# Scores of two attention mixers as stacked one-pass products, and rotations with one shuffle

## The chip, the cores and the metric

The kernel runs on one core of a Trainium2 chip. The metric is the device time of one execution in microseconds (us). Names of engines in the profile: PE is TensorE's matrix unit, PEld its weight loads, DVE VectorE, ACT ScalarE, POOL GpSimd, SP the engine that issues most transfers.

## The reference

A bidirectional encoder trunk with two layers, width 1024, on 256 grid tokens (4 rows by 64 columns) and 16 meta tokens, 272 in all. A layer is half a SwiGLU block, a mixer, and half a SwiGLU block again, each ahead of it an RMS norm. The mixer runs three attentions on one combined projection:

```python
def hybrid_mixer(n, w_in, sink, rpb, qn, kn, w_branch, w_out, pos, row, col):
    ...
    ang = rope_angles(pos, HEAD_DIM)
    oa = window_sink_attention(apply_rope(heads(qa, A_Q_HEADS), ang), apply_rope(heads(ka, A_KV_HEADS), ang),
                               heads(va, A_KV_HEADS), sink)
    ob = neighbourhood_attention(heads(qb, B_HEADS), heads(kb, B_HEADS), heads(vb, B_HEADS), rpb)
    qc = apply_axial_rope(rms_norm(heads(qc, C_Q_HEADS), qn), row, col)
    kc = apply_axial_rope(rms_norm(heads(kc, C_KV_HEADS), kn), row, col)
    oc = dense_block_attention(qc, kc, heads(vc, C_KV_HEADS))
    branches = jnp.stack([oa, ob, oc], axis=2)
    up = jnp.einsum('blnc,ncd->blnd', branches, w_branch)
    g = jax.nn.sigmoid(gates.reshape(B, L, N_BRANCH, D_MODEL))
    return jnp.sum(g * up, axis=2) @ w_out
```

A and C have 8 query heads and 2 key heads of 64 dimensions, B has 8 of each. A is a window of 128 positions with a sink logit per head, C is dense. apply_rope turns dimension d of the first half of a head with dimension d of its second half:

```python
    return jnp.concatenate([x1 * cos - x2 * sin, x2 * cos + x1 * sin], axis=-1).astype(x.dtype)
```

apply_axial_rope does the same in each half of a head (32 dimensions), by row and by column.

## The kernel before, in words

Tokens run along the free dimension (T = 272 columns; 256 in what follows the last layer's mixer inputs), features along the 128 partitions. Projections are made in three one-pass products (fp32r): weights and activations are each split into a rounded part (hi, xh) and the rest (lo, xl), and mm (L267 to L280) sums hi·xh, hi·xl and lo·xh into a tile acc. unit (L217) loads a block of weights of 4 x 128 rows by 256 columns (raw), ScalarE makes hi by a copy that rounds, and VectorE, in the mixer for every third block POOL, makes lo by a subtraction. With pairs=True it also reorders the columns so that one head of each key group lie next to each other: group g = 0 in partitions 0 to 63 of a projection's output, g = 1 in 64 to 127; then ScalarE works in two halves, and the rest is made half by POOL and half by VectorE (L232).

The mixer (L681) projects B's values, keys and queries first. Then weave (L861) runs an attention and, at each of its yields, one piece of other work: beside neighbourhood (B) the pieces a_keys, a_queries(0), a_queries(1) and c_keys, beside mix_a c_queries(0), c_queries(1) and three or four gated(1, mp), beside mix_c the gated(0, mp), and then gated(2, mp) and the output projection. A scheduler puts each engine's instructions in an order of its own, with the program's order as its guide; each engine then runs its queue in that order.

The queries of A and C are in one tile of 128 partitions x 4 heads x 272 (qa, qc), the keys in one of 128 x 272 (ka, kc), both in full fp32. grouped (L466) computes the scores: products (L474) makes four heads at a time, each by one fp32 product with 64 rows, which leaves two records on TensorE:

```python
                PE.matmul(s, q[g * HD:(g + 1) * HD, t, qi * 128:(qi + 1) * 128], kk[g * HD:(g + 1) * HD, :],
                          start=True, stop=True)
```

Each product writes one of three PSUM banks (bank("s", 3)), which transposes use too; a bank is free again when the softmax pass on VectorE (L402 in A and B, L407 in C) or, in C, ScalarE's exponential (L409) has read it. turned (L496) transposes the probabilities, values (L509) makes the weighted sums. There are 2 query blocks x 2 halves x 4 heads = 16 such products per mixer and layer. meta_products (L520) does the same for the 16 meta queries of all heads at once, in layer 0 only.

rope_a (L737) makes A's rotation: four products of 32 partitions each read one quarter of the projection and write it, times the sine, to the quarter that it is turned with (L742), one product with the cosine (L743), and POOL adds (L744). rope_c (L779) makes the tables from cosine, sine and gain on VectorE at each of its three calls (L783, L784), shuffles by 16 partitions within 32 (L785), and multiplies and adds on POOL and VectorE.

qk (L156) gives buffers of a pool with six of 128 x 1408, which biases, vb, kb, qb, qa, qc, the running sums of the gated branches (tot) and the split inputs of the output projection (halves) take in turn; scr (L113) gives one of five of 128 x 544.

## Time and profile before

| | us |
|---|---|
| median of 3 runs | 1351.46 (1351.28 to 1352.11) |
| profiled execution | 1346.27 |
| its span | 1344.5 |
| VectorE busy | 890.4 |
| ScalarE busy | 649.5 |
| POOL busy | 159.5 |
| attention of layer 0, from the transposes of B's values to the last weighted sum | about 248 to 430 |
| attention of layer 1, the same | about 926 to 1075 |

Busy times are of one profiled execution. A record on PE lasts about 0.29 us for a projection product, but these are pipelined: the next starts after about 0.125 us. What a product costs is therefore read from start to start, not from its duration. The timeline gives the start of each record from the start of the span; records of one line in a row are merged with their count.

### The profile page before, as it was taken

The page shows a single profiled execution, that of the slowest core. Times are in us where ns is not written, and L with a number is a line of the kernel's source. Part 1 is how long each engine was busy: PE and PEld are TensorE (multiplying, and loading weights), DVE is VectorE, ACT ScalarE, POOL GpSimd, SP SyncE. Part 2 cuts the span into 40 slices and gives each one's busy share as a digit, 9 for nine tenths or more (in the row PEclk, how much of TensorE's full clock was granted, in tenths as well). Part 3 has the DMA queues.
Part 4 walks back from the last instruction along what each step waited for, and adds up shares of the span by engine and source line. Part 5 has one row for each costly group of instructions (what it writes and reads, how often), then busy time and mean ns, then how long its engine had stood idle before and what let it go on. Part 6 is the DMA issues. An engine that isn't in the chain of part 4 may idle for free.

```text
span 1344.5 us, 25887 instructions
## 1 busy us (share of the span) xinstructions
PE 1326.9 (99%) x10683; PEld 1286.6 (96%) x10683; DVE 890.4 (66%) x1316; ACT 649.5 (48%) x937; POOL 159.5 (12%) x97
## 2 busy tenths in 40 slices
PE   9999999999999999999999999999999999999997
PEld 8999999988988999999999999999889999999997
DVE  6655669688564687646676646676886557765663
ACT  6443444455454455434455434454565545544444
POOL 1000001232122220000000000023321233000000
PEclk9999999998999999999999999999999999999998
DMA  7765556433334576555465555455334465566652
GB/s 231 209 185 174 181 169 191 141 107 95 110 112 125 171 201 185 175 178 179 156 192 173 173 176 179 157 180 157 110 95 122 122 180 184 182 189 188 188 173 78
DMA packets 239010, 217.52 MB, mean 162 GB/s; under 512 B 24804, under 2 KB 237980, under 8 KB 238764
## 3 DMA queue, kind: packets, MB, share of 16 engines
q1 hardware_dynamic: 238540, 215.20, 52.4%
q8 instruction: 84, 1.38, 0.4%
q10 hardware_dynamic: 352, 0.66, 0.1%
q14 instruction: 34, 0.28, 0.1%
HBM read 214.78 MB, written 1.05 MB: 161 GB/s over the span
## 4 chain that ended last, share of the span: by engine, by line
PE 93%; DVE 5%; ACT 1%; issue 1%; DMA 0%; ACTq 0%; DVEq 0%
PE acc L279 29%; PE acc L280 28%; PE acc L278 28%; PE s L479 2%; PE pv L437 2%; PE s L502 1%; DVE lo L235 1%; PE s L641 1%; PE pv L432 1%; DVE p L422 1%; PE s L653 1%; PE s L337 0%; DMA qk<-in_meta_tokens_dram 0%; DVE p L402 0%; ACT hi L234 0%
## 5 line engine op out<-in xcount | busy, mean ns | idle before, releaser
L234 ACT CAST hi<-raw 128x1024 fp32r<-128x1024 f32 (+1 forms) x390 | 402.6, 1033 | 564.6 <-PE acc L279 384.9
L279 PE MATMUL acc<-xl,hi 128*128 128x272 f32 (+1 forms) x2160 | 622.5, 288 | 0.0
L280 PE MATMUL acc<-xh,lo 128*128 128x272 f32 (+1 forms) x2160 | 620.2, 287 | 0.7 <-DVE lo L235 0.7
L278 PE MATMUL acc<-xh,hi 128*128 128x272 f32 (+1 forms) x2160 | 619.9, 287 | 0.6 <-DVE qk L722 0.6
L235 DVE TENSOR_TENSOR lo<-raw,hi 128x1024 fp32r<-128x1024 f32 (+1 forms) x352 | 428.2, 1217 | 216.3 <-ACT hi L234 215.9
L278 PEld LDWEIGHTS acc<-xh,hi 128*128 128x128 f32 x2160 | 408.2, 189 | 9.6 <-issue 7.1
L279 PEld LDWEIGHTS acc<-xl,hi 128*128 128x128 f32 x2160 | 406.9, 188 | 4.5 <-issue 4.1
L280 PEld LDWEIGHTS acc<-xh,lo 128*128 128x128 f32 x2160 | 407.0, 188 | 3.7 <-issue 2.5
L279 PE MATMUL acc<-hl,hi 128*128 128x272 f32 (+1 forms) x704 | 201.8, 287 | 0.0
L280 PE MATMUL acc<-hh,lo 128*128 128x272 f32 (+1 forms) x704 | 201.1, 286 | 0.0
L278 PE MATMUL acc<-hh,hi 128*128 128x272 f32 (+1 forms) x704 | 200.4, 285 | 0.0
L278 PEld LDWEIGHTS acc<-hh,hi 128*128 128x128 f32 x704 | 132.7, 188 | 0.1
L280 PEld LDWEIGHTS acc<-hh,lo 128*128 128x128 f32 x704 | 132.3, 188 | 0.0
L279 PEld LDWEIGHTS acc<-hl,hi 128*128 128x128 f32 x704 | 132.2, 188 | 0.0
L235 POOL TENSOR_TENSOR lo<-raw,hi 128x1024 fp32r<-128x1024 f32 x38 | 92.4, 2432 | 256.5 <-ACT hi L234 243.3
L332 POOL TENSOR_TENSOR ss<-ss,scr 128x544 f32<-128x544 f32 (+1 forms) x12 | 17.5, 1456 | 602.7 <-ACT scr L329 602.6
L278 PE MATMUL acc<-oh,hi 128*128 128x272 f32 (+1 forms) x192 | 54.6, 284 | 0.0
L279 PE MATMUL acc<-ol,hi 128*128 128x272 f32 (+1 forms) x192 | 54.6, 284 | 0.0
L280 PE MATMUL acc<-oh,lo 128*128 128x272 f32 (+1 forms) x192 | 54.4, 283 | 0.0
L384 DVE TENSOR_TENSOR scr<-acc,scr 128x544 f32<-128x544 f32 (+1 forms) x40 | 28.7, 716 | 31.0 <-PE acc L280 30.9
L287 DVE SCALAR_TENSOR_TENSOR h<-acc,h 128x544 f32<-128x544 f32 (+1 forms) x40 | 28.6, 714 | 28.2 <-PE acc L280 28.1
L381 DVE TENSOR_TENSOR scr<-acc,rstd 128x544 f32<-128x544 f32 (+1 forms) x40 | 28.6, 716 | 26.2 <-PE acc L280 26.2
(244 smaller groups left out, 1311.7 us busy)
## 6 DMA issues: line engine op xcount, KB each, us to landing
raw<-in_ffn_w_in_dram SPq DMA_DIRECT2D x176, 512.0 KB, 3.6
raw<-in_ffn_w_out_dram SPq DMA_DIRECT2D x80, 512.0 KB, 3.4
raw<-in_w_in_dram SPq DMA_DIRECT2D x80, 512.0 KB, 3.9
raw<-in_w_in_dram SPq DMA_DIRECT2D x32, 256.0 KB, 3.2
raw<-in_w_branch_dram SPq DMA_DIRECT2D x32, 256.0 KB, 4.0
raw<-in_w_out_dram SPq DMA_DIRECT2D x16, 512.0 KB, 3.8
raw<-in_ffn_w_out_dram SPq DMA_DIRECT2D x16, 256.0 KB, 2.7
raw<-in_w_branch_dram SPq DMA_DIRECT2D x8, 512.0 KB, 3.7
```

What stands on the lines that cost most here:

```text
L234: ACT.copy(hi[:, :n], raw[:, :n])
L235: lo_engine().tensor_tensor(lo[:, :n], raw[:, :n], hi[:, :n].bitcast(F32), op=ALU.subtract)
L278: PE.matmul(o, a, rh, start=k == 0, stop=False)
L279: PE.matmul(o, a, rl, start=False, stop=False)
L280: PE.matmul(o, b, rh, start=False, stop=k == len(rows) - 1)
L287: DVE.scalar_tensor_tensor(hv, a[:, :, :n], 0.5, hv, op0=ALU.mult, op1=ALU.add)
L332: (DVE if j == 3 else POOL).tensor_tensor(ss, ss, dst, op=ALU.add)
L381: DVE.tensor_tensor(g, gate, rb, op=ALU.mult)
L384: DVE.tensor_tensor(g, up, g, op=ALU.mult)
L422: DVE.tensor_tensor(p, p, den[:, :n, None].to_broadcast([128, n, p.shape[2]]), op=ALU.mult)
L437: PE.matmul(pv[g * HD:(g + 1) * HD, t * 128:(t + 1) * 128], a, b, start=vm is None and kt == 0, stop=kt == 1 and (vm is None or t == 3))
L479: PE.matmul(s, q[g * HD:(g + 1) * HD, t, qi * 128:(qi + 1) * 128], kk[g * HD:(g + 1) * HD, :], start=True, stop=True)
```

## The change

Scores of A and C. The queries are stacked into 128 rows: for key group g, the 64 rows of that group hold the rounded part (ScalarE) and the other 64 rows the rest (VectorE). The keys are kept as four tiles: for each group the rounded part in both halves of the rows, and the rest in both halves. Two one-pass products of 128 rows then give (hi + lo)·hi and (hi + lo)·lo of queries and keys. qa and qc become a tile for each query half, ka and kc the stacked tile; meta_products builds its queries in the same form, with zeros for the other group.

Rotation of A. The columns of A's query weights and key weights are reordered in unit (turned=True), so that the partitions that are turned with each other lie 16 apart within 32, and the tables cos_a and sin_a with them. rope_a then uses one shuffle and one product in place of four products. The weight splits of A are cut into four pieces for the reordered columns (16 columns in a run), two made by POOL and two by VectorE.

Rotation of C. ScalarE makes the tables, and the two query halves share one.

Order and buffers. c_keys moves ahead of the two a_queries. vb is taken from the pool ahead of the biases, the running sums take the buffers of B's turned values (vk), and A's table and C's table for queries have a buffer of their own (tab).

```diff
-    def unit(nk, loads, pairs=False):
+    def unit(nk, loads, pairs=False, turned=False):
...
+        if turned:
+            order = "k g t" if pairs else "k t g"
+            rv, hv, lv = (t[:, :n].rearrange(f"p ({o} {c}) -> p k t g a b c", k=nk, t=2, g=2, a=2, b=2)
+                          for t, o, c in ((raw, order, "b a c"), (hi, "k t g", "a b c"), (lo, "k t g", "a b c")))
+            for g in range(2):
+                for b in range(2):
+                    ts = slice(None) if pairs else 0
+                    h_, r_, l_ = hv[:, :, ts, g, :, b], rv[:, :, ts, g, :, b], lv[:, :, ts, g, :, b]
+                    ACT.copy(h_, r_)
+                    (DVE if g else POOL).tensor_tensor(l_, r_, h_.bitcast(F32), op=ALU.subtract)
+            if not pairs:
+                hv, rv, lv = (t[:, :n].rearrange("p (k c) -> p k c", k=nk)[:, :, 128:] for t in (hi, raw, lo))
+                ACT.copy(hv, rv)
+                lo_engine().tensor_tensor(lv, rv, hv.bitcast(F32), op=ALU.subtract)
...
+    def stack_q(qs, src):
+        n = src.shape[2]
+        for g in range(2):
+            own, other = slice(g * HD, (g + 1) * HD), slice((1 - g) * HD, (2 - g) * HD)
+            dst = qs[:, g, :, :n]
+            ACT.copy(dst[own], src[own])
+            DVE.tensor_tensor(dst[other], src[own], dst[own].bitcast(F32), op=ALU.subtract)
+
+    def stack_k(src):
+        ks = qk(4, T, dt=F32R)
+        for g in range(2):
+            own, other = slice(g * HD, (g + 1) * HD), slice((1 - g) * HD, (2 - g) * HD)
+            for rows in (own, other):
+                ACT.copy(ks[rows, g, :], src[own])
+            for rows in (own, other):
+                DVE.tensor_tensor(ks[rows, 2 + g, :], src[own], ks[own, g, :].bitcast(F32), op=ALU.subtract)
+        return ks
...
-                PE.matmul(s, q[g * HD:(g + 1) * HD, t, qi * 128:(qi + 1) * 128], kk[g * HD:(g + 1) * HD, :],
-                          start=True, stop=True)
+                for part in range(2):
+                    PE.matmul(s, q[half][:, g, i // 2, qi * 128:(qi + 1) * 128], kk[:, 2 * part + g, :],
+                              start=part == 0, stop=part == 1)
...
-            for qd in range(4):
-                s0, d0 = 32 * qd, 32 * (qd ^ 1)
-                DVE.tensor_tensor(t[d0:d0 + 32], src[s0:s0 + 32], bc(tab[s0:s0 + 32, 1, :n], m), op=ALU.mult)
+            DVE.stream_shuffle(t, src, swap16)
+            DVE.tensor_tensor(t, t, bc(tab[:, 1, :n], m), op=ALU.mult)
...
         def a_queries(half):
-            if not half:
-                qa[0] = q_tile()
-            a = proj(head_pairs(w, A_Q, half), n_out)
-            rope_a(qa[0][:, 2 * half:2 * half + 2, :n_out], a[:, :, :n_out], 2)
+            a = proj(head_pairs(w, A_Q, half, turned=True), n_out)
+            qf = scr()[:, :, :n_out]
+            rope_a(qf, a[:, :, :n_out], 2)
+            qa.append(qk(2, 2, T, dt=F32R))
+            stack_q(qa[half], qf)
...
-            tb = scr()
-            DVE.tensor_scalar(tb[:, 0, :], C("cos_c"), gcol[:, 56 + col:57 + col], None, op0=ALU.mult)
-            DVE.tensor_scalar(tb[:, 1, :], C("sin_c"), gshuf[:, col:col + 1], None, op0=ALU.mult)
+            if not tb:
+                tb.append(sb.tile([128, 2, T], F32, name=nm("tab"), tag="tab", bufs=1) if m == 2 else scr())
+                ACT.activation(tb[0][:, 0, :], C("cos_c"), AF.Copy, scale=gcol[:, 56 + col:57 + col])
+                ACT.activation(tb[0][:, 1, :], C("sin_c"), AF.Copy, scale=gshuf[:, col:col + 1])
...
-        others = [a_keys, lambda: a_queries(0), lambda: a_queries(1), c_keys]
+        others = [a_keys, c_keys, lambda: a_queries(0), lambda: a_queries(1)]
```

The order that the scheduler makes of it, at two places of layer 0. First TensorE at the third and fourth score of mixer A (s_3349 and s_3353 before, s_3406 and s_3411 after; acc is the projection of c_queries(0)). Before:

```order
L461 MATMUL s_3321<-cst,v_2755 16x128
L280 MATMUL acc_3385<-xh_192,lo_3378 128x272
L278 MATMUL acc_3385<-xh_192,hi_3377 128x272
L279 MATMUL acc_3385<-xl_193,hi_3377 128x272
L280 MATMUL acc_3385<-xh_192,lo_3378 128x272
L278 MATMUL acc_3385<-xh_192,hi_3377 128x272
L279 MATMUL acc_3385<-xl_193,hi_3377 128x272
L479 MATMUL s_3349<-k_2754,qk_2959 128x272
L479 MATMUL s_3353<-k_2754,qk_2959 128x272
```

After:

```order
L499 MATMUL s_3376<-cst,v_2754 16x128
L296 MATMUL acc_3443<-xl_193,hi_3435 128x272
L297 MATMUL acc_3443<-xh_192,lo_3436 128x272
L295 MATMUL acc_3443<-xh_192,hi_3435 128x272
L518 MATMUL s_3406<-qk_2937,qk_3211 128x272 x2
L518 MATMUL s_3411<-qk_2937,qk_3211 128x272 x2
```

The two scores have become two products each. Ahead of them, since the first two scores of the mixer, 44 projection products and one transpose stood before, 28 and one transpose stand now.

Second VectorE ahead of the same scores: the end of c_keys (scr_3264 and scr_3265, k_2760) and the set-up of A's values (vm) before.

```order
L457 TENSOR_TENSOR vm_3327<-s_3321,cst 128x128
L301 TENSOR_TENSOR scr_3264<-scr_3264 128x272
L457 TENSOR_TENSOR vm_3327<-s_3321,cst 128x128
L302 TENSOR_SCALAR scr_3264<-scr_3264 128x272
L457 TENSOR_TENSOR vm_3327<-s_3321,cst 128x128
L303 TENSOR_TENSOR scr_3265<-scr_3265,scr_3264 128x272
L457 TENSOR_TENSOR vm_3327<-s_3321,cst 128x128
L804 TENSOR_TENSOR k_2760<-k_2760,scr_3265 128x272
L402 ISA p_3338,sm_3339<-s_3341,cst,sm_3335 128x272
L402 ISA sm_3339 128x1
L463 COPY v_3333<-s_3321 16x128
```

After, from the end of the second projection of A's queries (acc_3277) on; qk_3332 is the stack of the second query half, the ISA row the first softmax pass, L501 the last reader of the bank that the third score takes:

```order
L784 STREAM_SHUFFLE scr_3327<-acc_3277 128x544
L786 TENSOR_TENSOR scr_3326<-acc_3277,tab_2850 128x544
L785 TENSOR_TENSOR scr_3327<-scr_3327,tab_2850 128x544
L248 TENSOR_TENSOR lo_3564<-raw_3562,hi_3563 128x8x64
L248 TENSOR_TENSOR lo_3573<-raw_3571,hi_3572 128x8x64
L491 COPY v_3380<-s_3376 128x256
L469 TENSOR_TENSOR qk_3332<-scr_3326,qk_3332 64x544 x2
L311 TENSOR_TENSOR ol_2341<-pv_3351,oh_2340 128x4x128
L495 TENSOR_TENSOR vm_3382<-s_3376,cst 128x128 x4
L419 ISA p_3393,sm_3394<-s_3396,cst,sm_3390 128x272
L419 ISA sm_3394 128x1
L501 COPY v_3388<-s_3376 16x128
```

The work of c_keys has gone from this place to one earlier in the queue, and the rotation and the stack of A's second query half stand there now.

More of the change, by code (lines that the diff above doesn't have):

```diff
@@ L51, in angles @@
         return (position[None, :].astype(np.float32) * inv[freq_index][:, None]).astype(np.float32)
-    ang = angles(pos, d % 32, 64)
+    da = d // 32 * 16 + d % 32 // 16 * 32 + d % 16
+    ang = angles(pos, da % 32, 64)
     cos_a = np.cos(ang.astype(np.float64))
-    sin_a = np.sin(ang.astype(np.float64)) * np.where(d < 32, 1.0, -1.0)[:, None]
+    sin_a = np.sin(ang.astype(np.float64)) * np.where(da < 32, -1.0, 1.0)[:, None]
     ang_r = angles(row, d % 16, 32)
@@ L246, in plain, with head_pairs @@
         return units
-    def head_pairs(w, c0, half):
+    def head_pairs(w, c0, half, turned=False):
         units = []
@@ L256, in head_pairs @@
                               src.rearrange("(k p) c -> p k c", p=128)))
-            units.append(unit(4, loads, pairs=True))
+            units.append(unit(4, loads, pairs=True, turned=turned))
         return units
@@ L520, in meta_products @@
         def meta_products():
-            qm = sb.tile([128, 4, META], F32, name=nm("qm"), tag="qm", bufs=1)
-            DVE.tensor_copy(qm, q[:, :, GRID:])
-            qm = qm.rearrange("p t j -> p (t j)")
+            qm = sb.tile([128, 2, 2, HD], F32R, name=nm("qm"), tag="qm", bufs=1)
+            POOL.memset(qm.bitcast(F32), 0.0)
+            for g in range(2):
+                for half in range(2):
+                    DVE.tensor_copy(qm[:, g, g, half * 32:half * 32 + 32].rearrange("p (t j) -> p t j", t=2),
+                                    q[half][:, g, :, GRID:])
             s = bank("s", 3)[:, :T]
             for g in range(2):
-                PE.matmul(s[g * HD:(g + 1) * HD, :], qm[g * HD:(g + 1) * HD, :], kk[g * HD:(g + 1) * HD, :],
-                          start=True, stop=True)
+                for part in range(2):
+                    PE.matmul(s, qm[:, g].rearrange("p a b -> p (a b)"), kk[:, 2 * part + g, :],
+                              start=g + part == 0, stop=g + part == 2)
             p = sb.tile([128, 1, T], F32, name=nm("pq"), tag="pq", bufs=1)
@@ L686, in mixer @@
             late_dma(sink, sink_a.partition_broadcast(128))
+        vb = qk(4, 2, KB)
         biases = [bias_load(l, qi) for qi in range(2)]
@@ L701, in kv_tile @@
             return sb.tile([128, T], F32, name=nm(tag), tag=tag, bufs=2)
-        vb, kb = qk(4, 2, KB), qk(4, 2, KB)
+        kb = qk(4, 2, KB)
         qb = q_tile()
@@ L739, in rope_a @@
             t = scr()[:, :m, :n]
-            for qd in range(4):
-                s0, d0 = 32 * qd, 32 * (qd ^ 1)
-                DVE.tensor_tensor(t[d0:d0 + 32], src[s0:s0 + 32], bc(tab[s0:s0 + 32, 1, :n], m), op=ALU.mult)
+            DVE.stream_shuffle(t, src, swap16)
+            DVE.tensor_tensor(t, t, bc(tab[:, 1, :n], m), op=ALU.mult)
             DVE.tensor_tensor(dst, src, bc(tab[:, 0, :n], m), op=ALU.mult)
             POOL.tensor_tensor(dst, dst, t, op=ALU.add)
-        ka, va = kv_tile("k"), kv_tile("v")
-        qa, qc = [None], [None]
+        va = kv_tile("v")
+        ka, kc, qa, qc = [], [], [], []
         def a_keys():
             nonlocal tab
-            tab = scr()
+            tab = sb.tile([128, 2, T], F32, name=nm("tab"), tag="tab", bufs=1)
             DVE.tensor_tensor(tab[:, 0, :], C("cos_a"), r, op=ALU.mult)
             DVE.tensor_tensor(tab[:, 1, :], C("sin_a"), r, op=ALU.mult)
-            a = proj(plain(w, 0, 8, A_KV))
-            rope_a(ka[:, None, :], a[:, 0:1, :T], 1)
+            a = proj(plain(w, 0, 8, A_KV, turned=True))
+            kf = scr()
+            rope_a(kf[:, 0:1, :], a[:, 0:1, :T], 1)
             DVE.tensor_tensor(va, a[:, 1, :T], r, op=ALU.mult)
+            ka.append(stack_k(kf[:, 0, :]))
         def a_queries(half):
-            if not half:
-                qa[0] = q_tile()
-            a = proj(head_pairs(w, A_Q, half), n_out)
-            rope_a(qa[0][:, 2 * half:2 * half + 2, :n_out], a[:, :, :n_out], 2)
+            a = proj(head_pairs(w, A_Q, half, turned=True), n_out)
[3 more added lines that the diff above has]
+            stack_q(qa[half], qf)
         def mix_a():
@@ L802, in c_keys @@
             rsqrt(rk[:, 0, :], v2[:, 0, :], v2[:, 1, :])
-            rope_c(kc[:, None, :], u[:, 0:1, :], 2 + l, 1)
-            DVE.tensor_tensor(kc, kc, rk[:, 0, :], op=ALU.mult)
+            kf = scr()
+            rope_c(kf[:, 0:1, :], u[:, 0:1, :], 2 + l, 1, [])
+            DVE.tensor_tensor(kf[:, 0, :], kf[:, 0, :], rk[:, 0, :], op=ALU.mult)
+            kc.append(stack_k(kf[:, 0, :]))
         def c_queries(half):
-            if not half:
-                qc[0] = q_tile()
             a = proj(head_pairs(w, C_Q, half), n_out)
@@ L827, in c_queries @@
                     DVE.tensor_copy(rqv[:, 16:17], a[:, 1, T:T + 1])
-            rope_c(qc[0][:, 2 * half:2 * half + 2, :n_out], u, l, 2)
+            qf = scr()[:, :, :n_out]
+            rope_c(qf, u, l, 2, tbq)
+            qc.append(qk(2, 2, T, dt=F32R))
+            stack_q(qc[half], qf)
             if half:
@@ L835, in mix_c @@
         def mix_c():
-            return grouped(2, qc[0], kc, vc, oh, ol, None, None, None, None, rq, not last)
+            return grouped(2, qc, kc[0], vc, oh, ol, None, None, None, None, rq, not last)
         tot, halves = [], []
         def gated(b, mp):
-            if not tot:
-                tot.extend(qk(4, T) for _ in range(2))
+            if b == 1:
+                tot.append(sb.tile([128, 2 * T], F32, name=nm("tot"), tag="vk", bufs=4).rearrange(
+                    "p (m t) -> p m t", m=2))
             if b == 2 and not halves:
@@ L852, in gated @@
             i, j = divmod(2 * mp, 4)
-            tt = tot[i][:, j:j + 2, :n_out]
+            tt = tot[mp][:, :, :n_out]
             DVE.scalar_tensor_tensor(tt if b == 1 else g, g, 1.0, a[:, :, :n_out], op0=ALU.add, op1=ALU.mult)
```

17 lines of the change are left out of this document (10 added, 7 removed).

## The prediction

> **What bounds the kernel now.** I read the page's engine line first, then the busy time by stage, then TensorE's timeline where the score products stand.
>
> ```profile
> PE 1326.9 (99%) x10683; PEld 1286.6 (96%) x10683; DVE 890.4 (66%) x1316; ACT 649.5 (48%) x937; POOL 159.5 (12%) x97
> ```
>
> TensorE is idle for 1344.5 - 1326.9 = 17.6 us. What shortens its own work shortens the kernel, unless the work around it becomes late. The next view is by stretch: span, PE, PEld, DVE, ACT and POOL busy, granted clock, DMA. The first two rows are projections alone (272 and 256 columns), the others the mixers of layer 0 (248 to 430) and of layer 1 (926 to 1075).
>
> ```profile
> 500.00:690.00 190.00, 190.00 (x1521) 190.00 (x1521) 121.24 (x131) 84.28 (x97) 2.84 (x2) 1.00 0.58 176
> 1160.00:1320.00 160.00, 160.00 (x1371) 160.00 (x1370) 101.87 (x109) 74.64 (x86) 0.00 (x0) 1.00 0.59 184
> 248.00:333.00 85.00, 82.40 (x641) 72.60 (x640) 70.34 (x183) 48.53 (x111) 24.34 (x16) 0.96 0.31 95
> 333.00:430.00 97.00, 96.18 (x760) 86.65 (x758) 54.12 (x114) 48.85 (x93) 21.06 (x11) 1.00 0.39 115
> 926.00:962.00 36.00, 35.97 (x294) 32.51 (x293) 28.95 (x71) 21.20 (x56) 9.77 (x8) 1.00 0.40 118
> 962.00:1000.00 38.00, 35.43 (x293) 30.43 (x291) 35.65 (x93) 24.08 (x51) 10.73 (x7) 1.00 0.33 97
> 1000.00:1075.00 75.00, 75.00 (x626) 67.57 (x623) 45.51 (x94) 41.33 (x80) 16.71 (x8) 1.00 0.41 121
> ```
>
> A one-pass (fp32r) product of 272 columns takes 190/1521 = 0.125 us, one of 256 columns 160/1371 = 0.117. In the first half of each mixer VectorE is nearly as full as TensorE: 70.3 of 85, then 35.65 of 38 us (94%) in layer 1. In the second half it is at 56 to 61%. So TensorE bounds everywhere, and VectorE is close behind in the first halves.
>
> **The change: TensorE.** There are 64 score products of A and C, two mixers in two layers of 16 each. Each leaves two records. The timeline's columns are start, duration, engine, line:
>
> ```profile
> 299.79 0.29 PE L279 MATMUL acc<-xl,hi 128*128 128x272 f32 x1
> 300.01 0.73 PE L479 MATMUL s<-k,qk 64*128 64x272 f32 x4
> 300.67 0.39 PE L280 MATMUL acc<-xh,lo 128*128 128x272 f32 x1
> 300.90 0.29 PE L278 MATMUL acc<-xh,hi 128*128 128x272 f32 x1
> 301.15 0.29 PE L280 MATMUL acc<-xh,lo 128*128 128x272 f32 x1
> 301.37 1.18 PE L479 MATMUL s<-k,qk 64*128 64x272 f32 x6
> 302.48 0.39 PE L278 MATMUL acc<-xh,hi 128*128 128x272 f32 x1
> 302.71 0.29 PE L279 MATMUL acc<-xl,hi 128*128 128x272 f32 x1
> 364.67 0.29 PE L279 MATMUL acc<-xl,hi 128*128 128x272 f32 x1
> 364.89 0.72 PE L479 MATMUL s<-k,qk 64*128 64x272 f32 x2
> 365.54 0.39 PE L280 MATMUL acc<-xh,lo 128*128 128x272 f32 x1
> 365.77 0.29 PE L278 MATMUL acc<-xh,hi 128*128 128x272 f32 x1
> ```
>
> A pair of scores between two projection products costs 300.90 - 299.79 - 2x0.125 = 0.86 us, a run of three 302.71 - 301.15 - 0.25 = 1.31, a single one 365.77 - 364.67 - 0.25 = 0.85. In each case about 0.1 is lost going in (0.22 to the next start, not 0.125) and 0.1 coming out. TensorE's program has 19 single runs, 4 of two, 11 of three and one of four (0.86 + 0.66): 16.2 + 3.4 + 14.4 + 1.5 = 35.5 us. Afterwards there are 128 one-pass products over the full 128 rows, of the same form as the projections: 128 x 0.125 = 16.0 us. **TensorE saves 19.5 us**, 0.305 per score. The change's new form is not in the trace; if the 35 runs keep their 0.2 us, the saving is 12.5, and that is its lower bound. I take the upper one, as a score then has rows, columns and type of a projection product and nothing is left to switch. The meta products of layer 0 (4 before, 8 after) are too few to count.
>
> [...]
>
> **The other engines, per layer.**
>
> ```profile
> L742 DVE TENSOR_TENSOR scr<-acc,scr 32x544 f32<-32x544 f32 x8 | 5.8, 720 | 2.8 <-PE acc L280 2.7
> L742 DVE TENSOR_TENSOR scr<-acc,scr 32x272 f32<-32x272 f32 x8 | 3.5, 437 | 1.9 <-PE acc L280 1.8
> L783 DVE TENSOR_SCALAR scr<-cst,gcol 128x272 f32<-128x272 f32 x6 | 4.0, 669 | 0.0
> L232 DVE TENSOR_TENSOR lo<-raw,hi 128x512 fp32r<-128x512 f32 x16 | 17.8, 1114 | 9.1 <-ACT hi L231 9.1
> L785 DVE STREAM_SHUFFLE scr<-scr 128x544 f32<-128x544 f32 x2 | 1.5, 767 | 0.0
> L299 DVE RECIPROCAL scr<-scr 128x272 f32<-128x272 f32 x2 | 3.7, 1840 | 0.0
> L402 DVE CUSTOM_DVE_ANT_0 p<-s,cst,sm 128x272 f32<-128x272 f32 x32 | 15.0, 490 | 0.7 <-PE s L479 0.7
> L294 DVE TENSOR_TENSOR qk<-qk,qk 128x544 fp32r<-128x544 f32 x4 | 2.9, 718 | 0.0
> L729 DVE TENSOR_TENSOR qk<-acc,rstd 128x256 f32<-128x256 f32 x8 | 3.0, 420 | 2.3 <-PE acc L280 2.3
> L457 DVE TENSOR_TENSOR vm<-s,cst 128x128 f32<-128x128 f32 x16 | 4.0, 276 | 0.0
> L293 ACT CAST qk<-qk 128x544 fp32r<-128x544 f32 x4 | 2.6, 650 | 2.5 <-DVE qk L858 2.5
> L298 ACT ACTIVATE scr<-scr 128x272 f32<-128x272 f32 x2 | 0.9, 430 | 0.0
> L202 ACT COPY h<-s 128x256 f32<-128x256 f32 x4 | 1.5, 402 | 0.1
> L231 ACT CAST hi<-raw 128x512 fp32r<-128x512 f32 x32 | 18.4, 618 | 21.7 <-PE acc L279 7.1 <-issue 5.9 <-PE acc L280 4.6
> ```
>
> (Line, engine, operation, tiles and shapes, count; then busy us, mean ns of one, idle time before.) VectorE loses 8 quarter products of 544 and 4 of 272 (7.5 us), 6 table products (all taken at L783's 0.67, its stalls included: 4.0) and 4 halves of A's weight splits (4.5): 16.0. It gains 3 shuffles (2 x 0.77 + 0.44) and 3 products (2 x 0.72 + 0.44; each operation of 272 that has no row here is taken at 0.44), 3.9 together, 8 stack subtractions of 544 (5.7) and 8 of 272 (3.5), and 8 weight pieces of 256 elements (3.4; strided pieces of 16 are not in the trace, so between this and L232's 1.114, 8.9): 16.5, about **half a us more**. The pieces of A's key and value weights (4 of 128 elements and two halves instead of two whole ones) come out even. ScalarE gains 8 x 0.65 + 8 x 0.43 for the stacks, 4 tables x 0.43, 16 pieces at 0.40 for 8 halves at 0.62 (1.4), and some 1.5 for the keys' weights: **some 13 us more**, on 97 of 182 us in layer 0 (48.5 + 48.9). The 85 us that it is idle there hide this; where they don't, each copy is a link of a chain (shuffle, product, POOL's sum, copy, subtraction) and counts in full.
>
> What counts is where this stands (the rows of order are shown with the change). c_keys moves ahead, with its two weight loads, past a_queries and its eight on SP; a_queries(1) stands next to mixer A's scores in its place, and the stack of the second query half stands on VectorE ahead of the first softmax. Before:
>
> ```profile
> 289.46 0.87 PE s L653 x8
> 290.94 0.73 PE acc L797 x4
> ```
>
> From here to the third score product (300.01 above) TensorE took 10.55 us, with 44 projection products. After, 28 stand there, the heads' product of c_keys (0.73) is gone and two scores cost 0.5 instead of 0.86: 10.55 - 16x0.125 - 0.73 - 0.36 = 7.5 us. VectorE must in that time do the shuffle 0.77, seven operations of 512 or 544 (5.0), one of 256 (0.42), five of 128 (1.4) and one softmax pass (0.49): 8.1 us, before it frees the third bank. So a wait of 0.6 us, some 0.3 more for the chain, and what VectorE is behind by (1 to 2 us, as c_keys' reciprocal of 1.84 and 3.5 us of key stacks now stand ahead of it). Behind that wait stand the next scores and the whole of c_queries. I put all such waits at **4 us per layer, 8 in all**, between 0 and 12.
>
> Against it stand waits that go. In layer 0, tables that VectorE made while POOL held it up (2.28 us once, over three times the mean), then a clock of half:
>
> ```profile
> 304.46 2.28 DVE L783 TENSOR_SCALAR scr<-cst,gcol 128x272 f32<-128x272 f32 x1
> 315.00:320.00 5.00, 5.00 (x23) 4.43 (x22) 3.68 (x9) 0.55 (x3) 1.34 (x1) 0.58 0.29 97
> 320.00:325.00 5.00, 5.00 (x35) 4.95 (x35) 3.98 (x12) 2.81 (x4) 1.08 (x1) 0.74 0.00 0
> ```
>
> TensorE is idle 2.6 us in 248:333 and 2.6 us in 962:1000, and the clock costs 5x0.42 + 5x0.26 = 3.4 us; I let the idle time go and half of the clock's price stay: 6 to 7 us. Net, the waits add some 2 us (bounds: -8 and +12). **Sum: 19.5 - 2 = 17.5 us.** The rest costs nothing: the running sums (tot) take buffers that mixer B's values have left; loads keep their number and size; POOL's 16 pieces replace 8 halves, on an engine that is busy 45 of 182 us. The stacks take the buffers of the biases: the second query half waits for the last score of B to be read, which stands ahead of it on VectorE in any case.
>
> **Rivals.**
> 1. *VectorE becomes the bound of both first halves.* For: 94% in layer 1 already. Then the 24 scores that lie there save nothing (24 x 0.305 = 7.3) and the waits come on top: 19.5 - 7.3 - 4 = 8 us, 1343. Against: the tables with their stall (2.28) and c_keys' reciprocal (1.84) leave the place where VectorE is fullest. 0.20.
> 2. *Slower: the stack subtractions meet POOL.* The same subtraction takes three times as long where POOL is at work:
>
> ```profile
> L294 DVE TENSOR_TENSOR qk<-qk,qk 128x512 fp32r<-128x512 f32 x4 | 8.5, 2130 | 2.8 <-ACT qk L293 2.8
> ```
>
> If all 16 per layer take 1.41 us more, that is 22.6 us; VectorE's idle time in 926:1000 (9.4) less what TensorE saves there and the added half covers some 5, so 18 are lost per layer: 1351.5 - 19.5 + 36 = 1368. It beats the gain from about 11 stalled ones per layer on. Against: POOL is busy 20.5 of 74 us there. 0.08.
> 3. *Stacking doesn't pay.* If weight loads set the pace (96% busy, one per record), their number stays (two per score), and so does the time: 1351. [...] Against: the pace follows the columns (0.125 and 0.117). 0.06.
> 4. *More:* no new waits, the old ones and the half clock gone: 19.5 + 5.2 + 3.4 = 28 us, 1323.5. 0.08.
>
> **How the numbers follow.** The profiled execution took 1346.3 us (span 1344.5 and 1.8 around it): 1346.3 - 17.5 = 1328.8. The runs' median is 5.2 us above it, so 1334.0. The forecast's own range is 1329 to 1339 (0.58). Taking in most of rivals 1 and 4 gives 1326 to 1345. A difference under 0.2% (2.7 us) can't be told from none: faster 0.86, same 0.06, slower 0.08.
>
> **What would show it.** Score records at 0.125 us from start to start with no gap before the projection that follows (else the bound 12.5 holds); the first halves at some 81 and 71 us instead of 85 and 74; VectorE's busy time within 5 us of 890; ScalarE's up by some 24; waits of TensorE on the softmax (L402 of before) between the second and third score of A, 2 to 4 us each. I would be wrong if those waits exceed 6 us per layer, or the half clock comes back in both layers.

## The result, and the profile after

| | before | after |
|---|---|---|
| median (range, runs) | 1351.37 us (1351.22 to 1352.11, 4) | 1339.09 us (1339.00 to 1340.89, 4) |
| profiled execution, its span | 1346.27, 1344.5 | 1339.12, 1337.3 |
| span less PE busy (TensorE idle) | 17.6 | 28.4 |
| half clock inside the two mixers | 6.8 | 3.4 |

The changed kernel takes 0.9924 of the time before, 95% interval 0.9907 to 0.9941: 12.3 us faster. The forecast was 1334.0 in a range of 1326 to 1345. The page's engine line of the changed kernel:

```profile
PE 1308.9 (98%) x10683; PEld 1285.8 (96%) x10683; DVE 903.7 (68%) x1352; ACT 671.4 (50%) x1009; POOL 170.4 (13%) x115
```

TensorE's busy time fell by 18.0 us, the span by only 7.2, since 10.8 us of new idle time stand against that. (Both profiles have some half clock: in e0 below, 5 us at a clock of 0.50 held 16 records instead of 35. As an estimate from that, half of it is taken as added busy time, 3.4 of 6.8 us before and 1.7 of 3.4 after. Without that, TensorE's work fell by 16.3 us.) VectorE has 13.3 us more, ScalarE 21.9. Where the idle time stands is read by stretch (span, then PE, PEld, DVE, ACT and POOL busy, granted clock, DMA):

```profile
500.00:690.00 190.00, 190.00 (x1522) 190.00 (x1521) 121.95 (x135) 85.42 (x98) 2.85 (x2) 1.00 0.57 177
248.00:333.00 85.00, 75.88 (x625) 68.65 (x626) 76.51 (x195) 58.71 (x139) 26.98 (x21) 1.00 0.30 90
333.00:430.00 97.00, 95.11 (x807) 91.46 (x803) 61.68 (x123) 49.35 (x95) 22.97 (x12) 1.00 0.43 126
926.00:962.00 36.00, 33.24 (x263) 29.74 (x262) 29.49 (x81) 25.59 (x68) 14.08 (x14) 0.98 0.30 87
962.00:1000.00 38.00, 34.52 (x296) 32.79 (x296) 34.79 (x86) 27.73 (x65) 12.05 (x7) 0.97 0.30 99
1000.00:1075.00 75.00, 75.00 (x684) 73.11 (x679) 48.53 (x101) 43.50 (x84) 16.76 (x8) 1.00 0.45 134
```

TensorE's idle time in the first half of layer 0's mixer is 9.1 us (2.6 before), in the second 1.9 (0.8), in the first half of layer 1's 2.8 + 3.5 (0.0 + 2.6); in the projections and in the last stretch there is none. VectorE is at 90% of the first half in layer 0 (76.51 of 85) and at 82 and 92% of the two stretches of that in layer 1 (29.49 of 36, 34.79 of 38), but at 64% of the second halves. Following one and the same projection product through both profiles, the changed kernel is level at 240 us, 1.6 behind at 333, 4.4 ahead at 430 and still at 926; then 0.2 behind at 962, 4.9 ahead at 1000, 7.2 ahead from 1063 to the end. So **the second halves win 6.0 and 2.3 us; the first lose 1.6 and win 0.5**.

The scores themselves do what was forecast. TensorE's timeline of the changed kernel, three scores in one run (start, duration, line):

```profile
335.11 0.29 PE L297 MATMUL acc<-oh,lo 128*128 128x272 f32 x1
335.24 0.91 PE L518 MATMUL s<-qk,qk 128*128 128x272 f32 x6
335.99 0.29 PE L295 MATMUL acc<-xh,hi 128*128 128x272 f32 x1
```

Six records from 335.24 to 335.99 are 0.125 us each, and 0.13 lies ahead of the first: nothing is lost going in or coming out here. The largest new waits, from the view of waits (engine, tile and line, what released it: us in total, times, longest):

```profile
PE s L541 <- DVE sm L419: 5.3, 3, 2.0
PE s L684 <- DVE sm L419: 3.9, 3, 1.9
```

Both are on the softmax pass, L419, which frees a PSUM bank. The second is where mixer B's next scores (L684) need it. VectorE's timeline there shows what stood ahead of the pass, the first row of TensorE's is what it had last done:

```profile
285.80 1.77 DVE L479 TENSOR_TENSOR qk<-scr,qk 64x272 fp32r<-64x272 f32 x4
287.60 0.72 DVE L785 TENSOR_TENSOR scr<-scr,tab 128x544 f32<-128x544 f32 x1
288.24 0.33 DVE L419 CUSTOM_DVE_ANT_0 p<-s,qk 128x176 f32<-128x176 f32 x1
286.49 0.29 PE L295 MATMUL acc<-xh,hi 128*128 128x272 f32 x1
288.64 0.56 PE L684 MATMUL s<-qk,qk 64*128 64x176 f32 x2 [1.86 <-DVE sm L419]
```

C's key stack (four subtractions, L479) and a product of A's rotation (L785) run while mixer B waits. The first wait, L541, stands behind operations of VectorE that took longer beside POOL's. VectorE, POOL and TensorE of the changed kernel at 307 us, and in the last row L439 once more, later and undisturbed:

```profile
307.06 3.44 DVE L439 TENSOR_TENSOR p<-p,sm 128x1024 f32<-128x1024 f32 x1
310.42 1.37 DVE L531 TENSOR_TENSOR pm<-p,sm 128x64 f32<-128x64 f32 x1
307.04 2.37 POOL L251 TENSOR_TENSOR lo<-raw,hi 128x1024 fp32r<-128x1024 f32 x1 [8.73 <-ACT hi L250]
309.37 2.34 POOL L835 TENSOR_TENSOR scr<-scr,tab 128x544 f32<-128x544 f32 x1
313.07 0.66 PE L541 MATMUL s<-cst,p 128*128 128x128 f32 x4 [2.02 <-DVE sm L419]
320.92 1.22 DVE L439 TENSOR_TENSOR p<-p,sm 128x1024 f32<-128x1024 f32 x1
```

L439, which takes 1.22 us at 320.92, took 3.44 where it started 0.02 us after POOL's first operation, and ended some 1.1 us after that; L531, which takes 0.22 us in most places, took 1.37 and ended 0.08 us after POOL's second. The softmax pass that the transposes (L541) wait for came behind both. The other two of these three waits look the same: the one at 326.87 us (1.58) comes behind an operation that the last section shows, the one at 992.78 us (1.70) behind

```profile
989.13 2.41 DVE L531 TENSOR_TENSOR pm<-p,sm 128x64 f32<-128x64 f32 x1
988.09 3.37 POOL L251 TENSOR_TENSOR lo<-raw,hi 128x1024 fp32r<-128x1024 f32 x1
```

where VectorE's operation of 64 columns ends at 991.54 us, 0.08 after POOL's.

### The profile page after: what moved, and what is told of

Read it like the earlier page. It is cut to its first block, busy times and chain, and to the rows that moved or that the text cites. A ratio compares the mean times of both kernels' runs of the same rounds, so it can differ in the third digit from the quotient of the medians.

```text
span 1337.3 us, 26009 instructions
## 1 busy us (share of the span) xinstructions
PE 1308.9 (98%) x10683; PEld 1285.8 (96%) x10683; DVE 903.7 (68%) x1352; ACT 671.4 (50%) x1009; POOL 170.4 (13%) x115
## 5 line engine op out<-in xcount | busy, mean ns | idle before, releaser
L250 ACT CAST hi<-raw 128x1024 fp32r<-128x1024 f32 (+1 forms) x386 | 398.6, 1033 | 551.6 <-PE acc L296 374.9
L401 DVE TENSOR_TENSOR scr<-acc,scr 128x544 f32<-128x544 f32 (+1 forms) x40 | 28.6, 716 | 31.0 <-PE acc L297 30.9
L304 DVE SCALAR_TENSOR_TENSOR h<-acc,h 128x544 f32<-128x544 f32 (+1 forms) x40 | 28.5, 714 | 28.4 <-PE acc L297 28.3
L398 DVE TENSOR_TENSOR scr<-acc,rstd 128x544 f32<-128x544 f32 (+1 forms) x40 | 28.6, 716 | 26.2 <-PE acc L297 26.2
```

The lines of the kernel that those rows point to most:

```text
L250: ACT.copy(hi[:, :n], raw[:, :n])
L304: DVE.scalar_tensor_tensor(hv, a[:, :, :n], 0.5, hv, op0=ALU.mult, op1=ALU.add)
L398: DVE.tensor_tensor(g, gate, rb, op=ALU.mult)
L401: DVE.tensor_tensor(g, up, g, op=ALU.mult)
```

## The experiments

Every kernel was timed beside the kernel before, in four batches; the changed kernel was timed in a batch of its own, so differences to it of 1 or 2 us are less sure than its runs' range says. TensorE idle is span less PE busy; half clock is the time inside the mixers in which the granted clock stood at 0.5 (after: one stretch of 3.41 us). Span, idle and half clock are of one profiled execution.

| kernel | median, us (range, runs) | ratio to before, 95% | span | idle | half clock |
|---|---|---|---|---|---|
| after | 1339.09 (1339.00 to 1340.89, 4) | 0.9924, 0.9907 to 0.9941 | 1337.3 | 28.4 | 3.4 |
| e0_before_again | 1350.15 (1344.88 to 1351.78, 10) | 1.0007, 0.9988 to 1.0025 | 1349.1 | 17.3 | 17.1 |
| e1_no_stack | 1342.79 (1340.15 to 1344.34, 5) | 0.9947, 0.9929 to 0.9965 | 1341.2 | 15.8 | 3.4 |
| e2_stack_only | 1352.83 (1351.89 to 1354.65, 10) | 1.0029, 1.0015 to 1.0043 | 1350.1 | 34.6 | 23.9 |
| e3_late_key_stack | 1336.10 (1335.40 to 1336.43, 4) | 0.9900, 0.9881 to 0.9919 | 1334.2 | 26.3 | 3.4 |
| e4_gate_first | 1335.85 (1334.35 to 1338.88, 4) | 0.9907, 0.9880 to 0.9935 | 1336.8 | 26.3 | 3.4 |
| e5_order_back | 1349.29 (1347.90 to 1350.17, 10) | 1.0002, 0.9988 to 1.0016 | 1347.6 | 32.0 | 23.9 |
| e6_quarters_back | 1350.07 (1347.98 to 1351.19, 10) | 1.0015, 1.0001 to 1.0028 | 1347.1 | 29.9 | 23.9 |
| e7_tables_back | 1337.62 (1337.39 to 1338.27, 4) | 0.9918, 0.9894 to 0.9943 | 1335.9 | 28.6 | 0 |
| e8_late_and_gate | 1332.48 (1331.93 to 1333.64, 4) | 0.9880, 0.9857 to 0.9902 | 1330.1 | 23.7 | 0 |
| e9_no_pool_early | 1339.78 (1339.59 to 1340.61, 4) | 0.9932, 0.9913 to 0.9951 | 1337.7 | 28.1 | 3.4 |
| e10_key_rest_pool | 1344.28 (1342.48 to 1345.93, 8) | 0.9963, 0.9948 to 0.9977 | 1342.8 | 29.9 | 17.1 |
| e12_mid_and_gate | 1332.63 (1332.04 to 1332.96, 4) | 0.9872, 0.9847 to 0.9897 | 1331.2 | 24.6 | 0 |

Theory came out in e0, and in the time in e3, e4 and e8; the rival's time came out in e1, e2 and e12. e5, e6 and e10 were slower than either side had said, e7 a little faster, and e9 fell between the two.

**e0_before_again** is the kernel before, unchanged, to see where the 5 us between its profiled execution and its median lie.

> The kernel before once more, unchanged. Its profiled execution took 1346.3 us where its timed runs took 1351.4; the changed kernel's took 1339.1 in both. Theory (a second level): the kernel before has executions at 1346 and at 1351, and the profiled one was of the lower kind; then this profile's span is either near 1344.5 or near 1349.6, and in the second case the trace shows where the 5 us stand (a longer stretch at half clock, or longer waits in the first half of a mixer). Rival (the profiler shifts it): the span is near 1344.5 again and timed runs stay at 1351.

One stretch of layer 1 in its profile (the windows' columns, as above):

```profile
977.00:982.00 5.00, 5.00 (x16) 3.25 (x15) 2.38 (x12) 3.51 (x11) 0.77 (x1) 0.50 0.00 2
```

The same stretch in the first profile of that kernel:

```profile
977.00:982.00 5.00, 5.00 (x35) 4.07 (x36) 3.84 (x15) 4.24 (x14) 1.28 (x1) 1.00 0.12 42
```

At a clock of 0.50 TensorE gets through 16 records where it had 35. Over the whole span the idle time is the same (17.3 and 17.6 us), the span 4.6 us longer, and 10.2 us more were run at half clock, which is worth 5.1 if half of that time is lost, an estimate. The loss lies in layer 1: up to 962 us this execution is even 0.9 us ahead. So the 5 us are no offset of the profiler: one and the same program takes 1344 to 1353 us, and the time goes with the granted clock. The executions of the kernel before beside the experiments say the same: of 57, the 15 with a mean granted clock of 0.996 or more took 1344.2 to 1347.3 us, the 20 with 0.992 or less 1350.3 to 1352.8.

**e1_no_stack and e2_stack_only** split the change: the first has the rotations, tables and the order of after with scores as before, the second the stacked scores alone.

```diff
e1  -                for part in range(2):
    -                    PE.matmul(s, q[half][:, g, i // 2, qi * 128:(qi + 1) * 128], kk[:, 2 * part + g, :],
    +                PE.matmul(s, q[g * HD:(g + 1) * HD, t, qi * 128:(qi + 1) * 128], kk[g * HD:(g + 1) * HD, :],
    ...
e2  -            DVE.stream_shuffle(t, src, swap16)
    +            for qd in range(4):
    ...
    -                ACT.activation(tb[0][:, 0, :], C("cos_c"), AF.Copy, scale=gcol[:, 56 + col:57 + col])
    +            DVE.tensor_scalar(tb[:, 0, :], C("cos_c"), gcol[:, 56 + col:57 + col], None, op0=ALU.mult)
    ...
    -        others = [a_keys, c_keys, lambda: a_queries(0), lambda: a_queries(1)]
    +        others = [a_keys, lambda: a_queries(0), lambda: a_queries(1), c_keys]
```

> The changed kernel with scores as before (fp32 products of 64 rows, no stacks); the shuffle, ScalarE's tables, the order and the buffers stay. Theory (the gain is TensorE's, 18 us of its work, and waits for VectorE take part of it back): TensorE's work is that of before, so 1348 to 1354 us, no faster than before by more than 3. Rival (the gain comes from what leaves VectorE, its quarter products and tables): 1339 to 1344, and stacking adds nothing.

> Stacked scores alone: A's quarter products and weight order, the tables on VectorE at each call and c_keys last, all as before; only the buffers (tot, tab, vb) are as in the changed kernel. VectorE then has about 20 us more to do than before. Theory (TensorE's 18 us, less waits in the first halves): between the changed kernel and before, 1339 to 1347, with TensorE idle over 30 us in the trace. Rival (VectorE has no room for stacks without the other edits): 1350 or more.

The engine line of e1:

```profile
PE 1325.4 (99%) x10683; PEld 1286.1 (96%) x10683; DVE 878.6 (66%) x1314; ACT 656.3 (49%) x977; POOL 164.3 (12%) x113
```

That of e2:

```profile
PE 1315.5 (97%) x10683; PEld 1289.1 (95%) x10683; DVE 906.9 (67%) x1354; ACT 664.2 (49%) x969; POOL 160.0 (12%) x99
```

And the stretch of layer 0 where e2 lost most:

```profile
290.00:333.00 43.00, 34.52 (x256) 30.34 (x257) 40.82 (x114) 29.11 (x66) 7.07 (x5) 0.84 0.23 69
```

Both came out as their rivals said. The parts don't add up: the rotations, tables and order alone gain 7 us, the stack alone nothing or a little less, both together 12. So more than half of the gain is there without the stack, and on top of the other edits the stack is worth 3.7 us (1342.79 to 1339.09). e1 leaves TensorE's work as it was (1325.4 less half of 3.4 is 1323.7; before, by the same sum, 1323.5); against e0 it wins 1.5 us of idle time, and, by the same estimate of half, some 6.8 by 13.7 us less of half clock; its five runs have mean granted clocks of 0.994 to 0.997, those of e0 0.991 to 0.997. That this clock gain comes from its edits, rather than from where its waits happen to fall, isn't shown. e2 shortens TensorE's work, but VectorE is busy 40.82 of 43 us, TensorE idle 8.5 us in that stretch alone, and 23.9 us run at half clock. So in this kernel stacking paid only together with the edits that relieve VectorE in the same first halves.

**e3_late_key_stack** moves C's key stack out of mixer B: it is made at the end of c_queries(1), from a buffer of its own.

```diff
-            kf = scr()
+            kf = sb.tile([128, 1, T], F32, name=nm("pq"), tag="pq", bufs=1)
...
-            kc.append(stack_k(kf[:, 0, :]))
+            kcf.append(kf)
...
+            if half:
+                kc.append(stack_k(kcf[0][:, 0, :]))
```

> The changed kernel with C's key stack made after the second half of C's queries, where it is needed, and not in c_keys, where its four subtractions stand on VectorE ahead of a softmax pass of mixer B that TensorE waits for (1.9 us in each layer). Theory (place on VectorE's queue): those two waits go, 2 to 4 us less, 1335 to 1337. Rival (VectorE is full in the first halves, whatever its order): the wait turns up later, 1338 to 1341.

It is 3.0 us faster than after, with 2.1 us less idle time; the wait L684 on the softmax is down from 3.9 us to 0.4, and L541 is now the largest:

```profile
PE s L541 <- DVE sm L419: 4.3, 3, 2.0
PE s L499 <- DVE vm L495: 2.0, 1, 2.0
```

So the key stack that stood ahead of mixer B's softmax was one of the new waits.

**e4_gate_first** puts projections of the gates between mixer A's score steps, ahead of c_queries, so that VectorE has more time there.

```diff
-        others += [lambda: c_queries(0), lambda: c_queries(1)]
-        others += [lambda mp=mp: gated(1, mp) for mp in range(4)]
+        others += [lambda: gated(1, 0), lambda: c_queries(0), lambda: gated(1, 1), lambda: c_queries(1)]
+        others += [lambda mp=mp: gated(1, mp) for mp in range(2, 4)]
```

> The changed kernel with two pieces of gated(1, mp) moved ahead of c_queries(0) and c_queries(1) beside mixer A, the same work in another order: TensorE gets 6 us of products at a place where VectorE is full, with little for VectorE to do. Theory (the changed kernel loses 11 us of waits because the first half of each mixer holds more of VectorE's work than the second, which has room): the waits on the softmax of mixer A shrink, TensorE idle goes from 28 to 20 to 24 us, 1331 to 1336. Rival (the waits come from chains inside one piece, not from VectorE's load): 1337 to 1341.

3.2 us faster than after by the median. (The profiled execution is its slowest, 1338.88, so the idle time and the half clock of its row are those of a run 3 us above the median.) Its largest wait is now the one that after has as well, L684 (after: 3.9 us), and L541 on the softmax (5.3) is no more among the eight largest:

```profile
PE s L684 <- DVE sm L419: 3.5, 3, 1.9
PE s L518 <- DVE sm L419: 2.0, 1, 2.0
```

The idle time fell less than that, to 26.3 us instead of the 20 to 24 expected, as new waits of 1 to 2 us came up. The wait at this place went as forecast; the gain in idle time was smaller.

**e5_order_back, e6_quarters_back and e7_tables_back** each undo one edit and keep the rest: the place of c_keys, the rotation of A by one shuffle (with the reordered rows), C's tables by ScalarE.

```diff
e5  -        others = [a_keys, c_keys, lambda: a_queries(0), lambda: a_queries(1)]
    +        others = [a_keys, lambda: a_queries(0), lambda: a_queries(1), c_keys]
e6  -            DVE.stream_shuffle(t, src, swap16)
    -            DVE.tensor_tensor(t, t, bc(tab[:, 1, :n], m), op=ALU.mult)
    +            for qd in range(4):
    +                s0, d0 = 32 * qd, 32 * (qd ^ 1)
    +                DVE.tensor_tensor(t[d0:d0 + 32], src[s0:s0 + 32], bc(tab[s0:s0 + 32, 1, :n], m), op=ALU.mult)
    ...
e7  -                ACT.activation(tb[0][:, 0, :], C("cos_c"), AF.Copy, scale=gcol[:, 56 + col:57 + col])
    +            DVE.tensor_scalar(tb[:, 0, :], C("cos_c"), gcol[:, 56 + col:57 + col], None, op0=ALU.mult)
    ...
```

> The changed kernel with c_keys behind the two a_queries again, as before. Theory (the order is what makes room: c_keys' reciprocal and key stack would stand ahead of mixer A's first scores): longer waits around the first scores of A and more half clock, 1341 to 1346. Rival (the order matters little, as VectorE is full in both places): 1337 to 1341.

> The changed kernel with A's rotation by four quarter products and the weights of A in their old order, split in whole blocks and halves. VectorE does 7.5 - 3.9 us more per layer for the rotation, the splits need fewer pieces. Theory (VectorE's load in the first halves sets the waits): 2 to 5 us slower than the changed kernel, 1341 to 1344. Rival (the cut-up splits cost what the shuffle saves): 1338 to 1340.

> The changed kernel with C's tables made on VectorE, at each of three calls per layer. VectorE does 4 us more per layer at most, two thirds of it just where mixer A's scores stand. Theory (VectorE's load there sets the waits, and a starved TensorE loses its clock): 2 to 5 us slower than the changed kernel and over 3.4 us at half clock in the trace, 1341 to 1345. Rival (tables fit into VectorE's gaps): 1338 to 1340.

Undoing the order or the rotation each costs nearly the whole gain, 10.2 and 11.0 us (beside the kernel before, ratios of 1.0002 and 1.0015); the tables nothing (e7 is even 1.5 us faster than after; TensorE is idle for 28.6 us and no half clock stands inside the mixers, so the loss of clock in its theory did not show). Of the 10.3 and 9.8 us by which their spans are longer than after's, idle time is 3.6 and 1.5. The rest, 6.7 and 8.3 us, is TensorE busy for longer on as many products as in after (10683 records), and goes with the clock: 23.9 us of half clock in both, 20.5 more than after (worth less than half of it, as TensorE was partly idle there). In e6 the waits on the softmax of mixer B (its L683 is L684 of after) are longer, one of them 3.2 us:

```profile
PE s L683 <- DVE sm L418: 6.3, 4, 3.2
```

**e8_late_and_gate** has the edits of e3 and e4 together.

> The late key stack and the gates ahead of C's queries together, in the changed kernel. Theory (both take work of VectorE out of the first half of the mixer, at places of their own): their gains of 3 us each add up, 1331 to 1334, TensorE idle 21 to 24 us. Rival (both shorten the same wait): 1335 to 1337, as each alone.

They add up: 3.0 and 3.2 alone, 6.6 together, TensorE idle 4.7 us less than after, no half clock inside the mixers, and the wait of L684 on the softmax halved (3.9 in after). At 1332.5 us it is the fastest kernel of the study, beside e12, 6.6 us ahead of after.

```profile
PE s L684 <- DVE sm L419: 2.0, 3, 0.9
PE s L696 <- ACT p L421: 1.7, 2, 1.1
```

**e9_no_pool_early and e10_key_rest_pool** ask what POOL does to VectorE. e9 takes the splits of whole weight blocks away from POOL until c_queries(1); e10 gives it C's and A's key rests.

```diff
e9  -            in_mixer[0] = dst is kb
    +            in_mixer[0] = False
    ...
    +            in_mixer[0] = bool(half)
e10 -                DVE.tensor_tensor(ks[rows, 2 + g, :], src[own], ks[own, g, :].bitcast(F32), op=ALU.subtract)
    +                POOL.tensor_tensor(ks[rows, 2 + g, :], src[own], ks[own, g, :].bitcast(F32), op=ALU.subtract)
```

> The changed kernel with POOL kept from whole blocks' rests until C's second query half; VectorE makes them. Some five blocks per layer of 1.2 us are added to VectorE's first half, and stalls of VectorE behind POOL's 2.4 us operations (2.2 us twice in layer 0, 2.2 and 0.8 in layer 1) leave it. Theory (VectorE's load): slower, 1341 to 1347, with half clock. Rival (the stalls behind POOL are what costs): 1332 to 1337.

> The changed kernel with the rest of the stacked keys (eight subtractions of 64 x 272 per layer) made by POOL instead of VectorE: 3.5 us per layer off VectorE. Theory (VectorE's load and order): the wait on mixer B's softmax goes, 1334 to 1337. Rival (POOL's operations hold VectorE up by as much): 1338 to 1342.

e9 settles nothing: POOL's busy time fell by 18 us, but the block at 307 us stayed on POOL and L439 took 3.44 us there as in after; the waits stayed too. e10 is 5.2 us slower than after. The 16 subtractions that left VectorE took 6.9 us, yet its busy time fell by only 3.3, and a wait on L439 that was 0.9 us grew to

```profile
PE s L696 <- DVE p L439: 5.3, 2, 2.8
```

So about half of the work moved from VectorE to POOL came back in longer operations of VectorE. Of the 5.5 us that the span grew, idle time is only 1.5; the other 4.0 go with the half clock, 17.1 us where after has 3.4. More POOL work at these places costs, but how much of after's own waits is POOL's part stays open.

**e12_mid_and_gate** is e8 with the key stack at the end of c_queries(0).

```diff
-            if half:
+            if not half:
```

> As e8_late_and_gate, with C's key stack behind the first half of C's queries instead of the second. In e8 the last layer's stack stood right ahead of mixer C's first scores, and TensorE waited 1.6 us there. Theory (place on the queue): that wait goes, no other comes, 1330.5 to 1332. Rival (VectorE is fuller at the first half's place, beside mixer A's softmax): 1332 to 1335, with the waits of mixer A longer.

0.15 us from e8, with the same idle time within 0.9 us: which half of c_queries the stack stands behind makes no difference that these runs show.

## Why the prediction was right, and where it was not

The direction, the engine that bounds and the range were right; the sum came out 5 us low, and two of its terms were wrong by 5 us or more, on opposite sides. That the time lies inside the range is in part luck. And the sum's whole gain was TensorE's work, where e1 shows 6.8 of the 12.3 us without any of that.

**TensorE saves 19.5 us: right in kind, a little large.** The new score record costs 0.125 us where its neighbours are ready and leaves no gap (335.11 to 335.99 us above), so the lower bound of 12.5 falls. That a switch of form cost the old runs their 0.2 us was the author's reading; the rows show the gap gone, not what made it. The work fell by 16.3 us in after, 16.9 and 17.0 in e12 and e8. Some 2 of the other 3 us are in the new records themselves: counted from each one's start to the next one's, or to its own end where that is sooner, the 128 take 18.1 us and not 16.0, as 20 of them, most the first of a run, take 0.2 us or more. Why these do, and where the rest is, stays open.

**New waits of 4 us per layer, net +2: the step that failed.** With 8 us of new waits and 5.2 of old idle time gone, TensorE's idle time was to grow by some 3 us; it grew by 10.8, and inside the mixers from 6.0 (2.6 + 0.8 + 2.6) to 17.3 us (9.1 + 1.9 + 2.8 + 3.5). It is inside the bound of +12, but far from the value chosen. Two things were mis-sized. First the place: the waits were put between the second and third score of A, on the softmax. There stand 0.7 us in layer 0 (ahead of the transpose L499 at 302.20 us) and 1.3 in layer 1 (ahead of the third score, 973.66), both on the set-up of A's values (L495); 3.9 us stand one place earlier, in mixer B, behind c_keys' stack, and 5.3 one place later, at the transposes of mixer A. e3 and e4 take up one of these each. Of the prediction's own signs of being wrong, neither is met as it was worded: the waits at its place stay below 6 us per layer, and half clock is in one layer only; but by all waits together layer 0 grew by 7.6 us (from 3.4 to 11.0). The forecast counted VectorE's work up to one score of A, and not what the moved piece does to the scores of mixer B, whose softmax passes stand behind it in the same queue. Second, VectorE's work:

**VectorE about +1 us in all: wrong.** It is +13.3 us. The stacks are near their prices (the 16 subtractions of 512 and 544 took 12.1 us instead of 11.5, those of 272 6.9 instead of 7). The weight pieces are not: 16 of 256 elements took 8.9 us instead of 6.8 (0.42 at the shortest, 0.95 at the longest), and 8 of 128 another 3.3, which the sum had let come out even. The largest part, some 8 us, wasn't counted at all: operations that the change leaves alone and that took longer. The largest group of these, 16 products, in the kernel before:

```profile
L492 DVE TENSOR_TENSOR pm<-p,sm 128x64 f32<-128x64 f32 x16 | 4.6, 289 | 0.0
```

The same group in the changed kernel, twice as long in the mean; its three long ones (1.37, 2.42 and 2.41 us) ran beside POOL, where before one did (1.37), and ten that met no work of POOL took 0.21 to 0.22:

```profile
L531 DVE TENSOR_TENSOR pm<-p,sm 128x64 f32<-128x64 f32 x16 | 9.0, 563 | 0.0
```

**ScalarE some +24 us: right** (21.9), and hidden: no wait on ScalarE over 1.7 us in total.

**The first halves at 81 and 71 us: wrong.** The first is as long as it was or longer (1.6 us behind at 333). The second takes 73.5 instead of 74 (from 4.4 ahead at 926 to 4.9 at 1000): by 962 it had lost all that layer 0 had won, and it won that back by 1000.

**The median 5.2 us above the profiled execution: wrong, and in the other direction.** The sum took it for a constant that the changed kernel has too. e0 shows it to go with half clock, of which two executions of the kernel before have 6.8 and 17.1 us inside the mixers. After's median is its profiled time, all of its runs lie within 1.9 us, and their mean granted clocks are 0.996 and 0.997. So some 5 of the 12.3 us are, by the estimate of half, clock that the changed kernel mostly doesn't lose, and the forecast had no term for that. That error hid most of the waits', by luck: profile to profile the change gives 7.2 us where 17.5 were forecast, and without the 5.2 added the forecast would have been 1328.8, 10 us low.

**The rivals.** Rival 1 (VectorE bounds the first halves, 1343) was the better picture of the mixers: they win next to nothing there, and the waits come on top; the time came out 4 us below its 1343, as the half clock went (3.4 us of it, where the executions of the kernel before have 6.8 and 17.1). Rival 2 (stack subtractions meet POOL) fell: of 16 large ones the median took 718 ns, the longest 1549; it was other operations that took longer beside POOL (L439 3.44 us, L531 2.42). Rival 3 (weight loads set the pace) fell too: PEld's busy time is the same within 0.8 us (1286.6 and 1285.8), and the time is not. Rival 4 was too good for this order, though e8 comes within 9 us of it.

## What to carry to other kernels

Where the next engine was 90% full in a stretch (VectorE for 76.5 of 85 us), work taken off the bounding engine there turned into waits (TensorE idle for 9.1 us instead of 2.6): shorten that engine's queue or change its order in the same stretch, and count every pass behind a moved piece, not only the one that it feeds. Edits of this kind need not add up (e3 and e4 did), so each is judged beside the others: stacking alone was worth nothing here, and without the new order or the new rotation the whole gain was gone. Before the profiled execution is taken as the base of a sum, its granted clock is compared with that of the other runs.
